# Prompt attention scores: the rotary query's high and low halves stacked on 128 partitions

## The chip, the cores and the metric

One core of a Trainium2 chip runs one inference step of one decoder layer as a single program. The metric is the device time of one execution, in microseconds (us); lower is better. The kernel before was timed in three runs, and one further execution was profiled.

## The reference

The layer has 512 prompt tokens and 8 sample sequences of 4 tokens each (544 columns in all). It runs a SwiGLU block, then two mixers side by side, a gated recurrence and a latent attention with 4 heads, then a second SwiGLU block. The change touches the prompt's scores of the latent attention alone. Its query has a part without position of 128 rows per head ("nope") and a rotary part of 64 rows per head; the rotary key of 64 rows is shared by all heads.

```python
qh = jnp.einsum('btc,chd->bthd', cq, w_q_up)
q_nope = qh[..., :QK_NOPE]                    # 128 per head
q_r = rope(qh[..., QK_NOPE:], pos)            # 64 per head
k_r = rope(kr[:, :, None, :], pos)[:, :, 0, :]  # 64, shared by the heads
...
s = (jnp.einsum('bqhr,bsr->bhqs', ql, c_kv) + jnp.einsum('bqhd,bsd->bhqs', qr, k_rope)) * scale
s = jnp.where(k_pos[None, None, None, :] <= qp[None, None, :, None], s, -jnp.inf)
p = jax.nn.softmax(s, axis=-1)
return jnp.einsum('bhqs,bsr->bqhr', p, c_kv)
```

For the prompt the kernel uses the expanded form: it computes keys and values of each head from the latent rows, so a score is nope query times nope key plus rotary query times rotary key.

## The kernel before

**Numbers in two halves.** A product of two float32 matrices is made of three products in a shorter float32 format (fp32r, shown as f32 by the profile). `split` makes a high half (a cast, on ACT, L168) and a low half (source minus high, on DVE, L169); for weights the same is done in L248 and L249. A product is then high·high + high·low + low·high; low·low is left out.

**The rotary query.** In the scope "at2" a loop over two head pairs g projects 128 rows (2 heads of 64), scales them into `qz` and calls `rope`. That copies four blocks of 32 rows into `rp_sw` with the halves swapped (ACT, L835), multiplies it (L836) and `qz` (L837) by the tables, and adds (L838, all DVE) into `qr`, 128 x 544. Then `split(qrh[:, g], qrl[:, g], qr)` gives the two halves, each with two heads on 64 partitions. Between these steps stand products for keys and values (accumulators `acc`, split by L168 and L169 into `uhb`/`ulb` and `Vh`/`Vl`).

**The rotary key.** The weight of the rotary key is loaded twice, so that `krT` holds the 64 rows on both halves of the partitions. Its halves are `Kh[:, 2]` and `Kl[:, 2]`.

**The scores.** `soft(hd, x)` makes the scores of head `hd` for half x of the prompt (256 queries): two groups, one for each tile of 128 queries. The group of query tile qt has N = 128·(qt+1) keys, so N is 128 and 256 for x = 0, and 384 and 512 for x = 1. With 4 heads there are 16 groups. A group is six products and one more: three of 128 rows (`qnh`, `qnh`, `qnl` against `Knh`, `Knl`, which lie in the buffers the profile calls `uhb` and `ulb`), three of 64 rows (`qrh`, `qrh`, `qrl` against `Kh`, `Kl`, called `ha` and `hb`), and a bf16 product with the identity (`idb`) that adds the causal mask `causb` (L1190). The first-named operand in a profile row s<-uhb,qnh is the one that streams; the query tile is the stationary weight. DVE then takes the maximum (L1195), ACT the exponential (L1199), PE transposes (`tp`, L1211), `split` makes `PTh`/`PTl`, and L1220 multiplies with the values into `o`.

**What sets the order.** A planner orders the instructions of each engine before the program is built; each engine then runs its list in order and waits on semaphores. Products of a later stage (projections, L257) are placed among the score groups. While heads of x = 0 end, `prep` weights (`w_q`, `wh`/`wl` of 128 x 768) are cast; while those of x = 1 run, output projections (`w_o`, 128 x 1024) and `decode_prep` (40 copies of `qsT`, half on ACT L1229, half on DVE L1231) run. After the last score group, gathers of cached pages start on POOL (L1354).

Of the kernel before, what the change touches and what calls it, by code (L numbers as in the profile page):

```python
# [9 lines left out]
F32R = mybir.dt.float32r  # L10
# [4 lines left out]
ALU = mybir.AluOpType  # L15
AX = mybir.AxisListType

P = 128
# [6 lines left out]
T = TP + TS  # L25
# [8 lines left out]
NH = 4  # L34
R = 256
RD = 64
# [72 lines left out]
def hybrid_step_kernel(  # L109
# [5 lines left out]
    nc = tc.nc  # L115
# [12 lines left out]
    def mk(shape, dt, tag, bufs=1, pool=None):  # L128
        return (pool or cur[-1]).tile(shape, dt, name=tag, tag=tag, bufs=bufs)

    @contextmanager
    def scope(name):
        with tc.tile_pool(name=name, bufs=1, reuse_waits="tile") as p_:
            cur.append(p_)
            yield p_
            cur.pop()
# [9 lines left out]
    def f32(ap):  # L146
        return ap.bitcast(F32)

    def actslot(name, x, dt=F32, shape=None, n=None):
        return mk(shape or [P, KD, n or HS[x]], dt, name + "ab"[x], pool=act)  # L150
# [13 lines left out]
    def gcol(j):  # L164
        return gv[:, j : j + 1]

    def split(hi, lo, src, eng=None):
        nc.scalar.copy(hi, src)  # L168
        (eng or nc.vector).tensor_tensor(lo, src, f32(hi), op=ALU.subtract)  # L169
# [603 lines left out]
    with scope("mix") as mx_:  # L773
# [39 lines left out]
        def more(n):  # L813
            for _ in some(n):
                pass
# [244 lines left out]
        with scope("at2"):  # L1060
            Vh = mk([P, 4, NH * P], F32R, "Vh")
            Vl = mk([P, 4, NH * P], F32R, "Vl")
            ukT = mk([P, NH, R], F32, "ukT")
            qrh = mk([P, 2, T], F32R, "qrh")
            qrl = mk([P, 2, T], F32R, "qrl")
            Q = [(qh[x], ql[x]) for x in BOTH]
            with scope("kv"):
                wkv = mk([P, 2, 1024], F32, "wkv")
                nc.sync.dma_start(wkv, w_kv.rearrange("(k p) f -> p k f", p=P))
                more(CQ[4])  # L1070
                s_kv = mk([P, T], F32, "s_kv")
                krT = mk([P, T], F32, "krT")
                for x, hs in enumerate(even):
                    nc.vector.tensor_tensor(krz[:, hs], krz[:, hs], U[x][2], op=ALU.mult)
                for x, hs in enumerate(even):
                    rstd(s_kv[:, hs], sumsq([zc[:, j, hs] for j in range(2)]), R, U[x][2])
                rope(krT, krz)
                ckT = mk([P, 2, T], F32, "ckT")
                for j in range(2):
                    nc.vector.scalar_tensor_tensor(ckT[:, j], zc[:, j], gcol(V_KVG + j), s_kv, op0=ALU.mult, op1=ALU.mult)  # L1080
                Kh = mk([P, 3, T], F32R, "ha", pool=act)
                Kl = mk([P, 3, T], F32R, "hb", pool=act)
                for j in range(3):
                    split(Kh[:, j], Kl[:, j], ckT[:, j] if j < 2 else krT)
                wk4 = wkv.rearrange("p k (h c) -> p k h c", h=NH)
                uk = mk([P, 2, 2, NH, P], F32R, "uk")
                for j in range(2):
                    split(uk[:, 0, j], uk[:, 1, j], wk4[:, j, :, :P])
                for g in range(2):
                    pu = ps("pu")  # L1090
                    for i in range(2):
                        for j in range(2):
                            nc.tensor.transpose(pu[:, (2 * i + j) * P : (2 * i + j + 1) * P], wk4[:, j, 2 * g + i, :P], ident)
                    nc.scalar.copy(ukT[:, 2 * g : 2 * g + 2], pu.rearrange("p (h r) -> p h r", h=2))
                more(9)
                uv = actslot("ul", 0, F32R, [P, 2, 2, NH * P])
                for j in range(2):
                    split(uv[:, 0, j].rearrange("p (h c) -> p h c", h=NH), uv[:, 1, j].rearrange("p (h c) -> p h c", h=NH), wk4[:, j, :, P:])
                Knh, Knl = (actslot(n, 1, F32R, [P, NH, TP]) for n in ("uh", "ul"))

                def keys(hd):
                    a = ps("acc", "acc")
                    mm3(a, [((uk[:, 0, j, hd], uk[:, 1, j, hd]), (Kh[:, j, :TP], Kl[:, j, :TP])) for j in range(2)])
                    split(Knh[:, hd], Knl[:, hd], a)

                def values(i):
                    a = ps("acc", "acc")
                    ts = slice(i * P, (i + 1) * P)
                    mm3(a, [((Kh[:, j, ts], Kl[:, j, ts]), (uv[:, 0, j], uv[:, 1, j])) for j in range(2)])
                    split(Vh[:, i], Vl[:, i], a)  # L1110

                for x in BOTH:
                    rstd(s_q[x], allsum(s_q[x]), QL, U[x][2])
                for g in range(2):
                    w = weight([w_qr[2 * g + i] for i in range(2)], KQ)
                    a = [gemm(w, Q[x]) for x in BOTH]
                    qz = mk([P, T], F32, "qz")
                    for x, hs in enumerate(even):
                        nc.vector.tensor_tensor(qz[:, hs], a[x], s_q[x], op=ALU.mult)
                    qr = mk([P, T], F32, "qr")  # L1120
                    rope(qr, qz)
                    split(qrh[:, g], qrl[:, g], qr)
                    for i in range(2):
                        nc.scalar.copy(qsT[0:RD, 2, :, :, 2 * g + i], qr[i * RD : (i + 1) * RD, TP:].rearrange("p (b t) -> p b t", b=NB))
                    keys(2 * g)
                    keys(2 * g + 1)
                for i in range(4):
                    values(i)
                po = ps("po")
                for j in range(2):  # L1130
                    nc.tensor.transpose(po[:TS, j * P : (j + 1) * P], ckT[:, j, TP:], ident)
                nc.vector.tensor_copy(cns, po[:TS, :R])
                nc.sync.dma_start(ckv_p, ckT[:, :, :TP])
                nc.sync.dma_start(kr_p, krT[0:RD, :TP])
                nc.sync.dma_start(ckv_s, cns)
                nc.sync.dma_start(kr_s, krT[0:RD, TP:])
                for j in range(2):
                    nc.vector.tensor_copy(kss[:, j], ckT[:, j, TP:])
                nc.vector.tensor_copy(kss[0:RD, 2], krT[0:RD, TP:])
# [26 lines left out]

            def soft(hd, x):
                qnh, qnl = qq[hd, x]
                r0 = (hd % 2) * RD
                q0 = 2 * x  # L1170
                ss = {}
                pe_t = mk([P, 896], F32, "pe", PEB)
                pes = {q0: pe_t[:, : (q0 + 1) * P], q0 + 1: pe_t[:, (q0 + 1) * P : (2 * q0 + 3) * P]}
                for qt in (q0, q0 + 1):
                    qs = slice(qt * P, (qt + 1) * P)
                    ls = slice((qt - q0) * P, (qt - q0 + 1) * P)
                    N = (qt + 1) * P
                    s = ss[qt] = ps("s")
                    n = 0
                    for j in range(2):  # L1180
                        if j == 0:
                            qa = (qnh[:, ls], qnl[:, ls])
                            ka = (Knh[:, hd, :N], Knl[:, hd, :N])
                        else:
                            qa = (qrh[r0 : r0 + RD, hd // 2, qs], qrl[r0 : r0 + RD, hd // 2, qs])
                            ka = (Kh[r0 : r0 + RD, 2, :N], Kl[r0 : r0 + RD, 2, :N])
                        for a_, b_ in ((0, 0), (0, 1), (1, 0)):
                            nc.tensor.matmul(s[:, :N], qa[a_], ka[b_], start=n == 0, stop=False, skip_group_check=True)  # L1188
                            n += 1
                    nc.tensor.matmul(s[:, qt * P : N], idb, causb, start=False, stop=True, skip_group_check=True)  # L1190
                for qt in (q0, q0 + 1):
                    N = (qt + 1) * P
                    s = ss[qt]
                    mx = mk([P, 1], F32, "mx", 2, pool=sb)
                    nc.vector.tensor_reduce(mx, s[:, :N], axis=AX.X, op=ALU.max)  # L1195
                    nc.vector.tensor_scalar_mul(mx, mx, -SCALE)
                    pe = pes[qt]
                    sm = mk([P, 1], F32, "sm", 2, pool=sb)
                    nc.scalar.activation(pe[:, :N], s[:, :N], AF.Exp, scale=SCALE, bias=mx, accum_out=sm)  # L1199
                    nc.vector.reciprocal(sm, sm)  # L1200
                    nc.vector.tensor_scalar_mul(pe[:, :N], pe[:, :N], sm)
                return pes
# [488 lines left out]
```

## Time and profile before

| what | value |
|---|---|
| median of three runs | 1271.8 us (1271.74 to 1272.26) |
| profiled execution | 1272.22 us, span 1270.4 us |
| mean granted TensorE clock | 0.994 |
| PE busy | 1250.7 us, 98% of the span, 12442 instructions |
| PE weight loads (PEld) | 1159.4 us, 91% |
| DVE / ACT / POOL busy | 982.6 / 741.2 / 75.9 us |
| score products of the prompt (L1188, L1190) | 112 products, between 629.2 and 701.2 us |

PE is the matrix engine, and PEld its weight loads, which overlap products; DVE, ACT, POOL and SP are the vector, scalar, general and DMA-issuing engines. A timeline row gives start and duration in us, engine, line, operation and out<-in; for PE then the tile, which is the part of the array that a product uses (rows*columns), and the shape of the streamed operand. "x2" joins neighbours of one kind, and brackets at the end give how long the engine stood idle before, and what it waited for. Ends of products are modelled and overlap the next start, so the cost of a product in a stream is read from start to start.

### The profile page before, as it was taken

How to read it: one execution, taken by the hardware profiler on the slowest of the kernel's cores; microseconds unless marked ns; L12 is line 12 of the kernel's file. 1: busy time of each engine (PE TensorE's matmuls, PEld its weight loads, DVE VectorE, ACT ScalarE, POOL GpSimd, SP SyncE). 2: the span in 40 equal slices, each digit the busy share in tenths (PEclk: the TensorE clock that was granted, in tenths of full speed). 3: DMA queues.
4: the chain of work that ended last, by engine and by line, in shares of the span. 5: the costliest groups of instructions: out<-in, count | busy, mean ns of one | idle time of the engine just before them, and what ended most of it. 6: DMA issues, size and time to landing. Idle time of an engine off the chain costs nothing.

```text
span 1270.4 us, 30188 instructions
## 1 busy us (share of the span) xinstructions
PE 1250.7 (98%) x12442; PEld 1159.4 (91%) x12442; DVE 982.6 (77%) x1972; ACT 741.2 (58%) x1560; POOL 75.9 (6%) x80
## 2 busy tenths in 40 slices
PE   8999999999999999999999999999999999999998
PEld 7999999999999988889888888788788999999996
DVE  7897778888678887767766898989987778566664
ACT  7665545454566644546557655664656776554454
POOL 0000000000000000000000422322300000000000
PEclk9999999999999999999999899999999999999998
DMA  6233323332254221223223978878676635545541
GB/s 233 84 117 100 100 84 100 101 100 92 54 218 157 78 90 59 80 78 127 80 85 102 345 254 298 286 263 316 240 267 209 193 113 178 189 133 187 157 144 49
DMA packets 73018, 195.08 MB, mean 154 GB/s; under 512 B 12368, under 2 KB 27760, under 8 KB 68144
## 3 DMA queue, kind: packets, MB, share of 16 engines
q1 hardware_dynamic: 64320, 149.88, 36.3%
q0 software_dynamic: 7168, 41.95, 9.0%
q8 instruction: 98, 1.61, 0.5%
q10 hardware_dynamic: 1392, 1.32, 0.4%
q14 instruction: 40, 0.33, 0.1%
HBM read 183.45 MB, written 9.67 MB: 152 GB/s over the span
## 4 chain that ended last, share of the span: by engine, by line
PE 88%; DVE 6%; ACT 5%; issue 1%; DMA 0%; SPq 0%; DVEq 0%; ACTq 0%
PE acc L257 29%; PE acc L275 18%; PE dn L257 8%; PE Y L559 6%; PE X L559 4%; PE Z L559 4%; PE s L1375 3%; PE acc L715 3%; PE o L1408 2%; DVE wl L249 1%; PE s L1188 1%; PE pa L931 1%; PE acc L286 1%; ACT wh L248 1%; DVE kh L1363 1%
## 5 line engine op out<-in xcount | busy, mean ns | idle before, releaser
L248 ACT CAST wh<-wraw 128x1024 fp32r<-128x1024 f32 (+2 forms) x194 | 185.1, 957 | 185.5 <-PE acc L257 117.9
L249 DVE TENSOR_TENSOR wl<-wraw,wh 128x1024 fp32r<-128x1024 f32 (+2 forms) x194 | 214.5, 1107 | 82.6 <-ACT wh L248 82.2
L275 PE MATMUL acc<-uha,wh 128*128 128x256 f32 (+1 forms) x528 | 159.3, 302 | 0.9 <-ACT uha L205 0.9
L275 PE MATMUL acc<-ula,wh 128*128 128x256 f32 (+1 forms) x528 | 151.5, 287 | 0.0
L275 PE MATMUL acc<-uha,wl 128*128 128x256 f32 (+1 forms) x528 | 150.3, 285 | 0.8 <-DVE wl L249 0.7
L257 PE MATMUL acc<-uhb,wh 128*128 128x288 f32 (+1 forms) x432 | 128.2, 297 | 0.0
L257 PE MATMUL acc<-ulb,wh 128*128 128x288 f32 (+1 forms) x432 | 127.5, 295 | 0.0
L257 PE MATMUL acc<-uhb,wl 128*128 128x288 f32 (+1 forms) x432 | 126.8, 295 | 0.6 <-DVE wl L249 0.3
L275 PEld LDWEIGHTS acc<-uha,wh 128*128 128x128 f32 x528 | 100.1, 190 | 15.2 <-issue 13.2
L275 PEld LDWEIGHTS acc<-uha,wl 128*128 128x128 f32 x528 | 100.1, 190 | 1.6 <-DVE wl L249 1.3
L275 PEld LDWEIGHTS acc<-ula,wh 128*128 128x128 f32 x528 | 100.5, 190 | 1.0 <-issue 1.0
L257 PEld LDWEIGHTS acc<-uhb,wl 128*128 128x128 f32 x432 | 81.2, 188 | 1.3 <-DVE wl L249 1.3
L257 PEld LDWEIGHTS acc<-uhb,wh 128*128 128x128 f32 x432 | 81.0, 187 | 0.7 <-ACT wh L248 0.3
L257 PEld LDWEIGHTS acc<-ulb,wh 128*128 128x128 f32 x432 | 81.1, 188 | 0.1
L257 PE MATMUL dn<-hh,dh 128*128 128x272 f32 x256 | 74.3, 290 | 0.0
L257 PE MATMUL dn<-hh,dl 128*128 128x272 f32 x256 | 73.7, 288 | 0.0
L257 PE MATMUL dn<-hl,dh 128*128 128x272 f32 x256 | 73.6, 288 | 0.0
L1399 ACT COPY pbuf<-pt 32x64 f32<-32x64 f32 x192 | 46.5, 242 | 13.3 <-DVE pt L1395 10.6
L1375 PE MATMUL s<-kh,q 64*32 64x128 f32 x2560 | 54.0, 275 | 0.0
L275 PE MATMUL acc<-uhb,wh 128*128 128x272 f32 x176 | 53.3, 303 | 0.0
L257 PE MATMUL acc<-hlb,wh 128*128 128x288 f32 x176 | 52.1, 297 | 0.0
L257 PE MATMUL acc<-hhb,wh 128*128 128x288 f32 x176 | 51.8, 298 | 0.0
(642 smaller groups left out, 3904.7 us busy)
## 6 DMA issues: line engine op xcount, KB each, us to landing
wraw<-w_u SPq DMA_DIRECT2D x66, 512.0 KB, 3.5
wraw<-w_g SPq DMA_DIRECT2D x65, 512.0 KB, 4.0
wraw<-w_d SPq DMA_DIRECT2D x40, 384.0 KB, 3.3
wraw<-w_in SPq DMA_DIRECT2D x24, 512.0 KB, 3.6
wraw<-w_d SPq DMA_DIRECT2D x32, 320.0 KB, 2.9
wraw<-w_d SPq DMA_DIRECT2D x16, 512.0 KB, 4.0
wraw<-w_o SPq DMA_DIRECT2D x16, 512.0 KB, 4.0
g_S<-state SPq DMA_DIRECT2D x4, 512.0 KB, 4.0
```

Of the source, the lines that this page charges most:

```text
L248: nc.scalar.copy(wh[:, :kt], w[:, :kt])
L249: nc.vector.tensor_tensor(wl[:, :kt], w[:, :kt], f32(wh[:, :kt]), op=ALU.subtract)
L257: nc.tensor.matmul(out, a, b, start=n == 0, stop=n == last)
L275: nc.tensor.matmul(acc[:, :n], a[:, k], b[:, k], start=k + i == 0, stop=k == kt - 1 and i == 2)
L286: nc.tensor.matmul(acc, a[:, k], b[:, k], start=k + i == 0, stop=k == kt - 1 and i == 2)
L559: nc.tensor.matmul(bank, a[p][:, k], b[q][:, k], start=first and k + n == 0, stop=k == 3 and n == 2, skip_group_check=True)
L715: nc.tensor.matmul(accs[x, d], wts[d][p][:, k], hs[k // 2][q][:, k % 2, x], start=k + n == 0, stop=k == nf - 1 and n == 2)
L931: nc.tensor.matmul(pa[es, c * 32 : (c + 1) * 32].rearrange("p (n m) -> p n m", m=m), kx[:, cs], up(qx[:, cs]), start=True, stop=True, skip ...
L1188: nc.tensor.matmul(s[:, :N], qa[a_], ka[b_], start=n == 0, stop=False, skip_group_check=True)
L1375: nc.tensor.matmul(self.s[r][c * 32 : c * 32 + 32, :P], q[rs, j], kh, start=st + jj == 0, stop=st == len(JS) - 1 and jj == 1, skip_group_c ...
L1399: (nc.scalar.copy if g else nc.vector.tensor_copy)(self.p[g * 32 : g * 32 + 32, c // 2, c % 2 * 4 : c % 2 * 4 + 4, self.i * 16 : self.i * ...
L1408: nc.tensor.matmul(o[g : g + 32, :R], self.p[:, c, a], self.craw[c][:, a], start=i + c == 0 and a < 4, stop=i + c == 2 and a >= 4, skip_gr ...
```

## The change

The tile pair `qrh`, `qrl` (each 128 x 2 x 544) is replaced by one tile `qr2` (128 x 4 x 544, the same size). For each head the cast writes the high half on the 64 partitions where its rows lie, and the subtract writes the low half on the other 64. As the key lies on both halves of the partitions, one product of 128 rows with `Kh` gives high·high + low·high, and one with `Kl` gives high·low + low·low. A group has two rotary products of 128 rows instead of three of 64, and a low·low term more.

```diff
-            qrh = mk([P, 2, T], F32R, "qrh")
-            qrl = mk([P, 2, T], F32R, "qrl")
+            qr2 = mk([P, NH, T], F32R, "qr2")
...
                     rope(qr, qz)
-                    split(qrh[:, g], qrl[:, g], qr)
+                    for i in range(2):
+                        a_, b_ = slice(i * RD, (i + 1) * RD), slice((1 - i) * RD, (2 - i) * RD)
+                        nc.scalar.copy(qr2[a_, 2 * g + i], qr[a_])
+                        nc.vector.tensor_tensor(qr2[b_, 2 * g + i], qr[a_], f32(qr2[a_, 2 * g + i]), op=ALU.subtract)
...
-                    for j in range(2):
-                        if j == 0:
-                            qa = (qnh[:, ls], qnl[:, ls])
-                            ka = (Knh[:, hd, :N], Knl[:, hd, :N])
-                        else:
-                            qa = (qrh[r0 : r0 + RD, hd // 2, qs], qrl[r0 : r0 + RD, hd // 2, qs])
-                            ka = (Kh[r0 : r0 + RD, 2, :N], Kl[r0 : r0 + RD, 2, :N])
-                        for a_, b_ in ((0, 0), (0, 1), (1, 0)):
-                            nc.tensor.matmul(s[:, :N], qa[a_], ka[b_], start=n == 0, stop=False, skip_group_check=True)
-                            n += 1
+                    kn, kr = ([t[:, j, :N] for t in ts] for ts, j in (((Knh, Knl), hd), ((Kh, Kl), 2)))
+                    qr = qr2[:, hd, qs]
+                    for a_, b_ in ((qnh[:, ls], kn[0]), (qnh[:, ls], kn[1]), (qnl[:, ls], kn[0]), (qr, kr[0]), (qr, kr[1])):
+                        nc.tensor.matmul(s[:, :N], a_, b_, start=n == 0, stop=False, skip_group_check=True)
+                        n += 1
```

The lines behind it move up, by four in `soft` and below (L1188 becomes L1184, L1190 becomes L1186, L1229 becomes L1225). On PE 16 products fall away. A group of N = 384 on PE, before:

```order
L1188 MATMUL s<-uhb,qnh 128x384
L1188 MATMUL s<-ulb,qnh 128x384
L1188 MATMUL s<-uhb,qnl 128x384
L1188 MATMUL s<-ha,qrh 128x384
L1188 MATMUL s<-hb,qrh 128x384
L1188 MATMUL s<-ha,qrl 128x384
L1190 LDWEIGHTS idb
L1190 MATMUL s<-causb,idb 128x128
```

The same group after (`qr_7262` is the tile `qr2`; the sizes here are those of the output):

```order
L1184 MATMUL s<-uhb,qnh 128x384
L1184 MATMUL s<-ulb,qnh 128x384
L1184 MATMUL s<-uhb,qnl 128x384
L1184 MATMUL s<-ha,qr_7262 128x384
L1184 MATMUL s<-hb,qr_7262 128x384
L1186 LDWEIGHTS idb
L1186 MATMUL s<-causb,idb 128x128
```

One rotary product is gone, and the causal product follows a product of 128 rows. The order of the other engines changes between some 615 and 705 us of the old trace. On DVE, around the first head pair's split, before:

```order
L838 TENSOR_TENSOR qr<-qr,rp_sw 128x544
L1119 TENSOR_TENSOR qz<-acc,s_q_4793 128x272
L1119 TENSOR_TENSOR qz<-acc,s_q_4794 128x272
L169 TENSOR_TENSOR qrl<-qr,qrh 128x544
L249 TENSOR_TENSOR wl<-wraw,wh 128x768
L837 TENSOR_TENSOR qr<-qz,trig 128x544
L836 TENSOR_TENSOR rp_sw<-rp_sw,trig 128x544
L169 TENSOR_TENSOR ulb<-acc,uhb 128x512
```

And after, the same place and the end of the stage:

```order
L838 TENSOR_TENSOR qr<-qr,rp_sw 128x544
L1118 TENSOR_TENSOR qz<-acc,s_q_4793 128x272
L1118 TENSOR_TENSOR qz<-acc,s_q_4794 128x272
L1124 TENSOR_TENSOR qr_7262<-qr,qr_7262 64x544 x2
L837 TENSOR_TENSOR qr<-qz,trig 128x544
L836 TENSOR_TENSOR rp_sw<-rp_sw,trig 128x544
L169 TENSOR_TENSOR ulb<-acc,uhb 128x512
L838 TENSOR_TENSOR qr<-qr,rp_sw 128x544
L169 TENSOR_TENSOR ulb<-acc,uhb 128x512
L169 TENSOR_TENSOR Vl<-acc,Vh 128x512
L1124 TENSOR_TENSOR qr_7262<-qr,qr_7262 64x544 x2
L169 TENSOR_TENSOR Vl<-acc,Vh 128x512 x3
```

Two subtracts of 64 rows stand for each one of 128, and the weight's `wl` has gone from here; it now stands behind the last `Vl` and the copy to `cns`, directly ahead of the first head's query. ACT's cast `wh` of the same weight moves with it. After that `wl` DVE now has two `ula` splits (128 x 256), the query half `qnl`, and two more `ula`; before, four `ula` came ahead of `qnl`.

On ACT, while the last groups of x = 1 are prepared (`qsT` copies are those of `decode_prep`, `wh` 128x1024 an output-projection weight), before:

```order
L1229 COPY q_8225<-qsT 32x128
L1199 ACTIVATE pe,sm<-s,mx 128x512
L1229 COPY q_8225<-qsT 32x128 x3
L248 CAST wh<-wraw 128x1024
L1229 COPY q_8225<-qsT 32x128 x3
L1222 COPY mb<-o 128x256
L768 COPY ma<-acc 128x256
L1238 COPY q_8225<-q_8225 32x10x16
L296 ACTIVATE ssp<-ma 128x256
L1238 COPY q_8225<-q_8225 32x10x16
L299 ACTIVATE ma<-ma,gv 128x256
L1238 COPY q_8225<-q_8225 32x10x16 x2
```

And after:

```order
L1225 COPY q_8218<-qsT 32x128
L1195 ACTIVATE pe,sm<-s,mx 128x512
L248 CAST wh<-wraw 128x1024
L768 COPY ma<-acc 128x256
L1225 COPY q_8218<-qsT 32x128
L296 ACTIVATE ssp<-ma 128x256
L1225 COPY q_8218<-qsT 32x128
L299 ACTIVATE ma<-ma,gv 128x256
L1218 COPY mb<-o 128x256
L1225 COPY q_8218<-qsT 32x128 x5
L1234 COPY q_8218<-q_8218 32x10x16 x4
L248 CAST wh<-wraw 128x1024
```

The weight cast comes ahead of three of the copies, and the copies go behind it; the set of instructions up to the next weight cast is the same. On PE the products that use these results move by a few places. POOL's order is the same, and on SP one store and one weight load change places.

More of the change, by code (lines that the diff above doesn't have):

```diff
@@ L1168, in soft @@
                 qnh, qnl = qq[hd, x]
-                r0 = (hd % 2) * RD
                 q0 = 2 * x
```

## The prediction

> **What bounds the kernel now.** I read the page first, its share of busy time and its chain, then the product timeline around the score groups, then the busy time of short stretches, and last PE's waits. From the page:
>
> ```profile
> PE 1250.7 (98%) x12442; PEld 1159.4 (91%) x12442; DVE 982.6 (77%) x1972; ACT 741.2 (58%) x1560; POOL 75.9 (6%) x80
> PE 88%; DVE 6%; ACT 5%; issue 1%; DMA 0%; SPq 0%; DVEq 0%; ACTq 0%
> ```
>
> PE is busy for 98% of the span and has 88% of the chain, so a microsecond that PE no longer needs is worth a microsecond, except in places where another engine ends last. The change touches PE from 629 to 701 us only. So I looked at that part in stretches (columns: length, then busy us and instructions of PE, weight loads, DVE, ACT and POOL, then the granted clock, DMA share and GB/s):
>
> ```profile
> 629.20:652.42 23.22, 23.22 (x181) 21.64 (x179) 14.49 (x46) 10.07 (x30) 0.00 (x0) 1.00 0.24 75
> 652.42:656.40 3.98, 3.86 (x30) 3.14 (x28) 3.90 (x13) 3.42 (x11) 0.63 (x1) 1.00 0.86 254
> 661.42:675.79 14.37, 13.32 (x93) 11.12 (x92) 11.81 (x40) 13.71 (x39) 0.00 (x0) 1.00 0.04 4
> 701.99:705.41 3.42, 2.38 (x16) 2.12 (x17) 2.39 (x8) 2.23 (x7) 2.81 (x4) 1.00 0.73 256
> 705.41:708.82 3.41, 1.94 (x15) 1.52 (x13) 2.54 (x5) 1.77 (x5) 2.94 (x3) 1.00 0.99 380
> 708.82:715.65 6.83, 6.41 (x29) 6.25 (x30) 6.69 (x15) 5.59 (x14) 2.02 (x3) 0.50 0.99 397
> ```
>
> From 629 to 652 PE has no idle time. In the next row DVE is full (3.90 of 3.98), and from 661.4 to 675.8 ACT is (13.71 of 14.37). There a shorter PE wins little. The last row matters for a rival: the clock is halved for 6.83 us.
>
> **What a score group costs now.** The product timeline of the two groups of the last head, N = 384 and 512 keys (start, modelled duration, tile, rows x columns):
>
> ```profile
> 698.20 0.34 PE L1188 MATMUL s<-uhb,qnl 128*128 128x384 f32 x1
> 698.47 0.44 PE L1188 MATMUL s<-ha,qrh 64*128 64x384 f32 x1
> 698.74 0.33 PE L1188 MATMUL s<-hb,qrh 64*128 64x384 f32 x1
> 698.92 0.34 PE L1188 MATMUL s<-ha,qrl 64*128 64x384 f32 x1
> 699.18 0.23 PE L1190 MATMUL s<-causb,idb 128*128 128x128 bf16 x1
> 699.22 0.48 PE L1188 MATMUL s<-uhb,qnh 128*128 128x512 f32 x1
> 699.54 0.39 PE L1188 MATMUL s<-ulb,qnh 128*128 128x512 f32 x1
> 699.77 0.39 PE L1188 MATMUL s<-uhb,qnl 128*128 128x512 f32 x1
> ...
> 701.05 0.39 PE L1211 MATMUL tp<-ident,pe 128*128 128x128 f32 x2
> ```
>
> The distance from one start to the next is what counts, since products overlap. Inside a run of equal tiles it is .18 at N = 384 (698.74 to 698.92) and .23 at 512 (699.54 to 699.77). Where the tile goes from 128*128 to 64*128 it is .27 (698.20 to 698.47), and again .27 behind the first 64-row product; where it goes back it is .26 (698.92 to 699.18). So each entry costs .09 + .09, and each exit .08 to .09. Rows do not shorten a product: 64 rows and 128 rows stream at the same distance. The small groups, N = 128 and 256:
>
> ```profile
> 629.37 0.28 PE L1188 MATMUL s<-uhb,qnl 128*128 128x128 f32 x1
> 629.57 0.32 PE L1188 MATMUL s<-ha,qrh 64*128 64x128 f32 x1
> 629.74 0.27 PE L1188 MATMUL s<-hb,qrh 64*128 64x128 f32 x1
> 629.85 0.27 PE L1188 MATMUL s<-ha,qrl 64*128 64x128 f32 x1
> 630.05 0.23 PE L1190 MATMUL s<-causb,idb 128*128 128x128 bf16 x1
> 630.09 0.36 PE L1188 MATMUL s<-uhb,qnh 128*128 128x256 f32 x1
> 630.29 0.28 PE L1188 MATMUL s<-ulb,qnh 128*128 128x256 f32 x1
> 630.41 0.29 PE L1188 MATMUL s<-uhb,qnl 128*128 128x256 f32 x1
> ...
> 631.22 0.50 PE L257 MATMUL acc<-q,wh 128*128 128x272 f32 x2
> ```
>
> Distances in stream: .11 at 128 (629.74 to 629.85), .12 at 256 (630.29 to 630.41).
>
> **Term 1, the groups.** After the change the three products qnl, stacked·ha, stacked·hb have one tile, and the causal product has it too. From the start of qnl to the start of what follows the causal product takes three stream distances and .04 (699.18 to 699.22):
> - N = 128: .72 (629.37 to 630.09) becomes .11×3 + .04 = .37, gain .35
> - N = 256: .81 (630.41 to 631.22) becomes .12×3 + .04 = .40, gain .41
> - N = 384: 1.02 becomes .18×3 + .04 = .58 (.56 unrounded), gain .45
> - N = 512: 1.28 becomes .23×3 + .04 = .73, with .03 for the wider step to the transposes .76, gain .52
>
> A head gains .76 in its first half (queries 0 to 255) and .97 in its second; four heads would be 6.9 us. One piece of this has no row: an f32 product of 128 rows followed by the bf16 causal product. The trace has only 64-row products ahead of it. Bounds: nothing extra (the step back from bf16 to f32 in one tile, .04), or all that the exit takes now, .09 ahead and up to .1 for uncovered weights. I take nothing, because its tile is 128*128 like its neighbours', and keep .2 for a rival. [...]
>
> **Term 2, the front.** The rotary queries are split twice, and the split now issues twice as many instructions:
>
> ```profile
> L168 ACT CAST qrh<-qr x2: 648/649/650, 615.7 to 622.3; 128x544 fp32r<-128x544 f32 x2
> L169 DVE TENSOR_TENSOR qrl<-qr,qrh x2: 714/720/726, 616.4 to 623.4; 128x544 fp32r<-128x544 f32 x2
> ```
>
> ```profile
> 611.11 2.61 ACT L835 COPY rp_sw<-qz 32x544 f32<-32x544 f32 x4
> 617.68 0.96 DVE L249 TENSOR_TENSOR wl<-wraw,wh 128x768 fp32r<-128x768 f32 x1 [0.54 <-ACT wh L248]
> 621.70 0.73 PE L257 MATMUL acc<-ula,ha 128*128 128x512 f32 x2 [0.39 <-DVE ulb L169]
> 626.16 1.07 DVE L169 TENSOR_TENSOR ula<-ma,uha 128x256 fp32r<-128x256 f32 x3
> 628.06 0.43 DVE L169 TENSOR_TENSOR qnl<-qn,qnh 128x256 fp32r<-128x256 f32 x1
> ```
>
> Four copies of 32 rows with 544 columns take 2.61, .65 each, as much as one of 128 rows. So a 64-row cast costs .65 and a 64-row subtract .72, and the change adds 2×.65 = 1.3 us on ACT and 2×.72 = 1.4 us on DVE between 615 and 624. A bound below would be half price, nothing added; above, I see no row dearer than these. The order moves a 768-wide weight's cast and subtract behind this place. On ACT that lets the second head pair's swap copies start some .2 to .3 earlier (a cast of .8 less, one of .65 and a start more), and on DVE the first pair's added .72 lies where .96 of the moved subtract and its wait of .54 were. So the wait of .39 at 621.70 shrinks by about .28 (ends 0 and .39). DVE then runs without a gap up to the first group's query half qnl, which ends at 628.49. Ahead of it come .72 (the second pair's added subtract) and the moved .96, behind it go two of the four output splits of .33 each: 628.49 + .72 + .96 − .66 − .28 = 629.23. PE first uses qnl at 629.37, with the .28 at 629.09: a wait of .14. I book the front at −.28 + .14 = −.14, with ends −.39 and +.4 (the .28 not won, and qnl that much later). The moved weight is needed at 631.6 and ready some 4 us before: 0, and the same 4 us are the cover. SP and POOL issue nothing more, and no DMA is added; SP's one swap, a store of the sample rows and a weight load far ahead of its use, I book at 0.
>
> **Term 3, what of term 1 arrives.** Heads 0 to 2, first halves, lie in the stretch without idle time: −3×.76 = −2.28. Head 3's first half lies beside the DVE-full stretch (652.4 to 656.4): its .76 is absorbed, PE would only wait longer for DVE. Then:
>
> ```profile
> 657.79 0.32 PE o L1220
> 658.11 0.54 PE s L1188 x2
> ```
>
> ```profile
> 661.42 0.27 ACT L1165 COPY qsT<-qa 128x64 f32<-128x64 f32 x1 [0.42 <-PE qa L1164]
> ```
>
> ```profile
> 666.67 0.66 PE L1211 MATMUL tp<-ident,pe 128*128 128x128 f32 x4 [0.36 <-ACT ma L1222]
> 668.74 0.39 PE L1220 MATMUL o<-PTh,Vh 128*128 128x256 f32 x1 [0.57 <-ACT PTh L168]
> 678.15 0.38 PE L257 MATMUL acc<-uha,wl 128*128 128x256 f32 x1 [0.35 <-DVE wl L249]
> ```
>
> The first two rows are of the chain, then ACT's timeline and PE's. Head 0's second half runs there, with an output product inside the 64-row run, which pays the switch twice more (.32 instead of .12 for it, .27 instead of .18 behind it: .3). So the 384 group gives .45 + .3 = −.75. From 661.42 ACT ends last: it waited .42 there, and then its work runs through (13.71 of 14.37, the rest being gaps of .03 between instructions). The .52 of the 512 group lets ACT start earlier by at most that wait: −.42. Head 1's second half (661.7 to 665.8) then only lengthens PE's waits at 666.67 and 668.74; its .97 is absorbed. The order shifts some of ACT's copies behind a weight cast, but the set up to the next cast (675.8) is the same, so that cast ends no later; DVE's half follows at 678.15 and PE goes on from there. Heads 2 and 3, second halves, lie in PE's stream (680 to 684, 697.9 to 701.1): −2×.97 = −1.94.
>
> Behind 701 PE waits for exp, its transpose and its split, a chain of fixed length that starts with the last group, and the gather on POOL starts with the last score product too:
>
> ```profile
> POOL ulb L1354 <- PE s L1188: 47.1, 1, 47.1
> ```
>
> So the tail moves as a whole, and from 709 to the end PE is the bound. The sum: −.14 −2.28 −.75 −.42 −1.94 = −5.53. The profiled execution took 1272.22; that gives 1266.7, and against the median of the runs (1271.8, .4 less) 1266.3.
>
> **Rivals.**
> (a) *The causal product still drains.* For: no row shows that pair. Against: it has the same tile. Of the 16 groups 11 count above (three first halves with two each, one, two second halves with two each), at .09 to .2: 1.0 to 2.2 us back, 1267.3 to 1268.5.
> (b) *The halved clock goes.* The clock fell at 708.82 behind two stretches of 3.4 us in which PE was busy 2.38 and 1.94, and came back after 6.83. Granted clock seems to follow how busy PE was in stretches of 3.4 us; if these waits, moved by 5.5 us, spread over three of them, each is busier, and up to half of 6.83 comes back: 3.4. Against: DMA is at .99 of its share there, so the weights behind would end last, and I expect 0 to 2 of it: 1264.3 to 1266, at best 1262.9. [...]
> (c) *The change doesn't do what it says*: the .27 steps belong to the query buffer, not to the tile, and only the 16 products go. Against: the step back to bf16 shows it too. Then 3×(.11+.12) + .18 + 2×(.18+.23) = 1.7 arrives, with the front and ACT's wait 2.3: 1269.5 to 1270.1, no change that one can tell.
> (d) *Slower: the clock is halved in the ACT-full stretch.* Heads 0 and 1 leave about 1.1 us more idle time on PE between 661 and 676 (.97 and .1), on top of 1.05 (14.37 less 13.32 busy). Busy falls from .93 to .85; the halving at 708 followed .70 and .57. Halved work of PE costs half its length, so it decides from 11 us on (2×5.5): the 6.83 seen, three times over, from 657 to 677, would cost 10.2 and give 1276.5. Far from the rows, a small chance.
>
> **How the numbers follow.** My forecast, .53: 1266.3, its own range 1265 to 1267.2. (a) .17, (b) .18, (c) .09, (d) .03. About .2%, 2.5 us, is what a measurement of this kernel can tell from no change, so the line lies at 1269.3. (a), (b) and the forecast are faster (.88); (c) is the same (.09); (d) slower (.03). The range leaves out (c), (d) and the best end of (b): 1263.0 to 1269.0.
>
> **What the profile of after should show.** No 64*128 tile in the score rows; five products a group; steps of .18 throughout at N = 384, and .58 or less from qnl to the product behind the causal one. The step ahead of the causal product decides (a). The wait of PE at 621.70 falls to about .1, with about as much at the first group. PE's waits at 666 and 668 grow to about 2 us together, and the start of the wait-free stream behind 678 comes 3.6 us earlier, the last score product 5.5 us earlier. The clock rows from 700 to 716 decide (b), those from 661 to 678 (d). I would be wrong by most if the DVE-full stretch moved on with PE, or ACT's copies, now behind the cast, made PE wait longer than the absorbed gains.

## Result: faster by 0.2%, 3.2 us instead of 5.5

The changed kernel takes 1268.51 us (median of 14 runs, 1266.72 to 1270.88), the kernel before 1271.67 (14 runs): ratio 0.9978, 95% interval 0.9971 to 0.9985 (the quotient of the two medians, 0.9975, lies inside). The profiled execution of the change took 1267.03 us, 1.5 less than the median; that of before was 0.6 above its median. So the two traces differ by 5.2 us and the medians by 3.2, and the difference between these two numbers is the subject of what follows. From the page of after:

```profile
PE 1243.1 (98%) x12426; PEld 1155.6 (91%) x12426; DVE 982.9 (78%) x1974; ACT 742.1 (59%) x1562; POOL 79.0 (6%) x80
PE 86%; DVE 6%; ACT 5%; issue 1%; DMA 1%; SPq 0%; DVEq 0%; ACTq 0%
```

PE has 16 products fewer and is 7.6 us less busy; the span is 5.1 us shorter, and the rest became waits. The product timeline of the last two groups in after:

```profile
694.16 0.33 PE L1184 MATMUL s<-uhb,qnl 128*128 128x384 f32 x1
694.33 0.33 PE L1184 MATMUL s<-ha,qr 128*128 128x384 f32 x1
694.50 0.34 PE L1184 MATMUL s<-hb,qr 128*128 128x384 f32 x1
694.68 0.23 PE L1186 MATMUL s<-causb,idb 128*128 128x128 bf16 x1
694.72 0.48 PE L1184 MATMUL s<-uhb,qnh 128*128 128x512 f32 x1
...
695.27 0.40 PE L1184 MATMUL s<-uhb,qnl 128*128 128x512 f32 x1
...
695.96 0.23 PE L1186 MATMUL s<-causb,idb 128*128 128x128 bf16 x1
696.03 0.94 PE L1207 MATMUL tp<-ident,pe 128*128 128x128 f32 x7
```

From qnl to what follows the causal product it is .56 at N = 384 and .76 at 512, as worked out. The step from the 128-row f32 product to the bf16 causal product is .18 (694.50 to 694.68), a stream step, where before took .26 behind a 64-row product (698.92 to 699.18): rival (a), .09 to .2 more there, is refuted. The first group and PE's waits up to 676 us:

```profile
621.99 0.73 PE L257 MATMUL acc<-ula,ha 128*128 128x512 f32 x2 [0.33 <-DVE ulb L169]
629.55 0.27 PE L1184 MATMUL s<-ulb,qnh 128*128 128x128 f32 x1
629.84 0.33 PE L1184 MATMUL s<-uhb,qnl 128*128 128x128 f32 x1
...
661.71 0.38 PE L1216 MATMUL o<-PTh,Vh 128*128 128x256 f32 x1 [0.26 <-ACT pe L1195]
664.05 0.65 PE L1207 MATMUL tp<-ident,pe 128*128 128x128 f32 x4 [0.74 <-ACT ma L1218]
673.83 0.38 PE L257 MATMUL acc<-uha,wh 128*128 128x256 f32 x1 [0.35 <-ACT wh L248]
675.10 0.39 PE L257 MATMUL acc<-uha,wl 128*128 128x256 f32 x1 [0.76 <-DVE wl L249]
```

The wait at 622 hardly shrank (.33 after .39), and the first qnl comes .18 late (.29 behind the product ahead of it, instead of .11). From 661 to 676 PE waits 2.1 us in four places; before it was 1.3 in three, up to 678 (.36, .57 and .35, shown in the prediction). Most of the gain of head 1 went there.

The causal products mark the stages. The first one starts at 630.05 before and 630.23 after, the last at 700.98 and 695.96: the stage is 70.93 and 65.73 us long, 5.20 less. Both starts of the program differ by .34 (an early product, 605.12 and 605.46), so up to the last score product the change wins 5.36. The forecast had 5.53.

### The profile page after: what moved, and what is told of

The parts are those of the page before. It is cut to its first block, busy times and chain, and to the rows that moved or that the text cites. A ratio compares the mean times of both kernels' runs of the same rounds, so it can differ in the third digit from the quotient of the medians.

```text
span 1265.3 us, 30161 instructions
## 1 busy us (share of the span) xinstructions
PE 1243.1 (98%) x12426; PEld 1155.6 (91%) x12426; DVE 982.9 (78%) x1974; ACT 742.1 (59%) x1562; POOL 79.0 (6%) x80
## 4 chain that ended last, share of the span: by engine, by line
PE 86%; DVE 6%; ACT 5%; issue 1%; DMA 1%; SPq 0%; DVEq 0%; ACTq 0%
PE acc L257 30%; PE acc L275 17%; PE dn L257 8%; PE Y L559 6%; PE X L559 4%; PE Z L559 4%; PE acc L715 3%; PE s L1371 3%; PE o L1404 2%; DVE wl L249 1%; ACT wh L248 1%; PE pa L931 1%; DMA wraw<-w_g 1%; PE acc L286 1%; DVE kh L1359 1%
```

## Experiments

The kernels ran on three chips: on one (the chip of the parts and of the copies on POOL; the first result took the same time) the kernel before takes 1271.6, on the two others 1283.4 and 1282.6 (there the decode stage takes 250 to 252 us instead of 239 to 240). Ratios are always to runs of the kernel before on the same chip.

**How the two kernels spread.** No edit.

> The kernel before, unchanged, to see how its own runs spread. Theory 1 (the halved clock behind the last score group is the cause of the spread): its runs fall into groups by granted clock, 0 to 3 stretches of 3.4 us halved, each worth about 1.7 us, and most of them have the two stretches of the profile (clock 0.994): spread about 1270 to 1273, ratio 1.000. Theory 2 (the spread is the start and the DMA, not the clock): span and granted clock are not related.

> The changed kernel, unchanged. Theory 1: ratio 0.997 to 0.998 again, spans of 1264.7 at clock 0.997 up to 1268 at 0.993, so the spread of 4 us goes with the clock, and the profile shows a number of halved stretches between 697 and 715 us that fits its own span. Theory 2: spans of one clock differ as much as spans of different clocks.

Measured: 1.0001 (0.9992 to 1.0010) and 0.9976 (0.9966 to 0.9986). The stage from the first to the last causal product was 70.89 and 65.73 us. Time goes with clock, though not in steps as neat as theory 1 had it: in 35 runs of before on the chip where it takes 1271.6 the correlation of span and granted clock is -0.81 (spans 1267.8 to 1270.3 at 0.997 to 0.999, 1270.3 to 1273.1 at 0.993 and 0.994); on the chip of these two runs it is only -0.48.

**Unused products in PE's waits.** In `value`, ahead of the output products:

```diff
                 o = ps("o")
+                with tc.issue_after(last_tp.ins) if x and hd > 1 else nullcontext():
+                    for _ in range((0, 0, 5, 4)[hd] * x):
+                        nc.tensor.matmul(o, Vh[:, 0, hs], Knh[:, hd], start=True, stop=True, skip_group_check=True)
```

> The changed kernel with nine products of 512 columns whose result is not used, five between the last-but-one head's transposes and its first output product, four at the same place of the last head, where PE waits 1.25 and 0.96 us in the profile. Theory 1: the two 3.4 us stretches there are busy enough, the halved clock goes in most runs, the median falls by 1 to 2 us to about 1266.7, and the spread to about 1 us. Theory 2: the products lie in waits, so the median stays at 1268.5 with the same spread; if they are in the way, up to 0.5 us slower.

> The kernel before with the same nine unused products. Theory 1: its two halved stretches go too, 1271.7 falls to between 1268.5 and 1270, and the distance to the changed kernel with the same products is what the score groups alone are worth, 5 to 5.7 us if the halved clock is gone from both, or about 3.2 us if it costs both the same. Theory 2: stays at 1271.7.

Measured: 0.9967 (0.9955 to 0.9979) with the change, 1.0002 (0.9993 to 1.0011) without it. Theory 1 fails in its times: without the change nothing was won, though no run of 11 had a clock below 0.9955, and with the change the median is only 0.4 us under the change's own on that chip (1.0 when it was repeated on the third), which the intervals do not tell from nothing. One reason stands in the trace: the five products did not fill the first wait. The timeline of a later run of the same kernel:

```profile
698.26 1.42 PE L1215 MATMUL o<-uhb,Vh 128*128 128x512 f32 x5 [1.25 <-ACT pe L1195]
```

They need no probabilities and yet waited 1.25 us for ACT's exponential, which reads a score tile. The author took it that they wait for the buffer of `o`, which a score tile held until then; no run shows which buffer it is. The products behind them lie on the path. In the kernel before the same five products waited .72 us, for DVE's maximum (L1196) and not for ACT; the maximum reads a score tile too.

**The change in parts.** Three edits: the stacked product by the low key issued twice (to the change); the third rotary product left out (to before); each split in two pieces of 64 rows (to before).

```diff
-...(qr, kr[0]), (qr, kr[1])):
+...(qr, kr[0]), (qr, kr[1]), (qr, kr[1])):
```

```diff
-                        for a_, b_ in ((0, 0), (0, 1), (1, 0)):
+                        for a_, b_ in ((0, 0), (0, 1), (1, 0))[: 3 - j]:
```

```diff
-                    split(qrh[:, g], qrl[:, g], qr)
+                    for i in range(2):
+                        a_ = slice(i * RD, (i + 1) * RD)
+                        split(qrh[a_, g], qrl[a_, g], qr[a_])
```

> The changed kernel with the stacked product by the low key issued twice, so three rotary products of 128 rows (the low key counts twice in the scores). The number of products is that of before, the tile switch is gone. Theory A (what is won at the last score product arrives whole at the end): the last causal product starts 3.5 to 3.7 us earlier than before (5.36 of the change less 1.7 for the products) and the time falls by as much. Theory B (some 1.5 to 2 us of any gain are given back behind the last score product, since work there does not start earlier with it): 3.6 us earlier at the last score product, about 2 us at the end. Rival C (the buffer, not the tile, made the .27 steps): no gain at all.

> The kernel before without the third rotary product, low query by high key (that term is left out): two rotary products of 64 rows in a group, the tile switch stays, and so does the old split. Theory A: 1.7 us earlier at the last score product and 1.7 us at the end. Theory B: 1.7 at the last score product, 0 to 1 at the end. Rival C: 5 us, as in the change.

> The kernel before with each rotary split made in two pieces of 64 rows, written to the old tiles, three products of 64 rows as before: the change's cost on ACT and DVE alone, with its moved weight cast. By the prediction 0 to 0.4 us slower at the first score group (-0.14 was booked with a wait of 0.14 at the first group); theory A: the same at the end, so a ratio of 1.0000 to 1.0003; theory B: no difference at the end.

Measured, stage from the first to the last causal product and ratio:

| kernel | stage, us | won | ratio |
|---|---|---|---|
| no tile switch, same count | 68.38 | 2.55 | 0.9981 (0.9973 to 0.9990), median -2.2 us |
| two products, switch stays | 68.86 | 2.07 | 1.0003 (0.9994 to 1.0012), median +0.2 us |
| split in pieces | 70.86 | .07 | 0.9999 (0.9990 to 1.0008), median +0.1 us |

Rival C is out: without the tile switch, and with as many products as before, the last score product comes 2.55 us earlier. The expectation of 3.6 there was too high; the two parts add up to 4.62, .58 less than the change, and where that is lost was not traced. Neither theory holds for both: by the medians the first kernel keeps what it won, the second loses it all. So the loss is not the same for every gain ahead of the tail; the kernels differ in something. PE's first two waits behind the last group, in the kernel without the switch and in that with two products:

```profile
701.28 0.36 PE L1216 MATMUL o<-PTh,Vh 128*128 128x256 f32 x1 [0.90 <-DVE mx L1192]
701.84 0.39 PE L1216 MATMUL o<-PTl,Vh 128*128 128x256 f32 x1 [0.21 <-DVE PTl L169]
```

```profile
701.70 0.38 PE L1220 MATMUL o<-PTh,Vh 128*128 128x256 f32 x1 [1.25 <-ACT pe L1199]
702.54 0.39 PE L1220 MATMUL o<-PTl,Vh 128*128 128x256 f32 x1 [0.46 <-DVE PTl L169]
```

And the same in before, and then in after with the two waits that follow:

```profile
702.80 0.36 PE L1220 MATMUL o<-PTh,Vh 128*128 128x256 f32 x1 [0.81 <-DVE mx L1196]
703.38 0.39 PE L1220 MATMUL o<-PTl,Vh 128*128 128x256 f32 x1 [0.23 <-DVE PTl L169]
```

```profile
698.21 0.38 PE L1216 MATMUL o<-PTh,Vh 128*128 128x256 f32 x1 [1.25 <-ACT pe L1195]
699.06 0.39 PE L1216 MATMUL o<-PTl,Vh 128*128 128x256 f32 x1 [0.46 <-DVE PTl L169]
702.77 0.39 PE L1216 MATMUL o<-PTh,Vh 128*128 128x256 f32 x1 [0.96 <-ACT PTh L168]
704.91 0.79 PE L275 MATMUL acc<-uha,wh 128*128 128x256 f32 x2 [0.93 <-ACT uha L205]
```

The change and the two-product kernel wait 1.71 us in the first two; before waits .81 + .23 = 1.04, the kernel without the switch 1.11. DVE's timeline shows why. Before:

```profile
699.01 1.22 DVE L249 TENSOR_TENSOR wl<-wraw,wh 128x1024 fp32r<-128x1024 f32 x1 [1.29 <-ACT wh L248]
700.15 0.42 DVE L298 TENSOR_TENSOR ssp<-ssp,sq 128x256 f32<-128x256 f32 x1
700.49 0.55 DVE L1195 TENSOR_REDUCE mx<-s 128x1 f32<-128x384 f32 x1
701.25 0.69 DVE L1195 TENSOR_REDUCE mx<-s 128x1 f32<-128x512 f32 x1 [0.21 <-PE s L1190]
...
702.09 0.56 DVE L169 TENSOR_TENSOR PTl<-tp,PTh 128x384 fp32r<-128x384 f32 x1
...
702.64 0.69 DVE L169 TENSOR_TENSOR PTl<-tp,PTh 128x512 fp32r<-128x512 f32 x1
```

After:

```profile
694.95 0.56 DVE L1191 TENSOR_REDUCE mx<-s 128x1 f32<-128x384 f32 x1 [1.27 <-PE s L1186]
695.42 1.21 DVE L249 TENSOR_TENSOR wl<-wraw,wh 128x1024 fp32r<-128x1024 f32 x1
696.56 0.42 DVE L298 TENSOR_TENSOR ssp<-ssp,sq 128x256 f32<-128x256 f32 x1
...
696.96 0.68 DVE L1191 TENSOR_REDUCE mx<-s 128x1 f32<-128x512 f32 x1
697.55 0.54 DVE L169 TENSOR_TENSOR PTl<-tp,PTh 128x384 fp32r<-128x384 f32 x1
...
698.32 0.68 DVE L169 TENSOR_TENSOR PTl<-tp,PTh 128x512 fp32r<-128x512 f32 x1
```

With shorter groups the planner put the first maximum ahead of a weight's low half (`wl`, `ssp`), 1.5 us of work that DVE ended .5 us before the last causal product, and ends .9 us behind it now. DVE first waited 1.27 us for PE; then the maximum of the last group starts 1.00 us behind its causal product (.27 before), and the previous head's two splits into PTl end 3.04 behind it (2.35 before). The kernel with two products has the same order; its maximum starts .71 behind the causal product (699.45), and its splits too end 3.04 behind it:

```profile
698.15 0.56 DVE L1195 TENSOR_REDUCE mx<-s 128x1 f32<-128x384 f32 x1 [1.56 <-PE s L1190]
698.62 1.21 DVE L249 TENSOR_TENSOR wl<-wraw,wh 128x1024 fp32r<-128x1024 f32 x1
...
700.16 0.68 DVE L1195 TENSOR_REDUCE mx<-s 128x1 f32<-128x512 f32 x1
```

In the change the order is only a part of it, though. `wl` needs ACT's `wh`. Where DVE waited for that, `wl` started 1.08 us behind the start of `wh`, and in after `wh` started at 693.88:

```profile
697.93 1.05 ACT L248 CAST wh<-wraw 128x1024 fp32r<-128x1024 f32 x1 [0.54 <-PE acc L257]
```

```profile
693.88 1.05 ACT L248 CAST wh<-wraw 128x1024 fp32r<-128x1024 f32 x1 [0.54 <-PE acc L257]
```

So `wl` could not have started before 694.96, where the first maximum starts now. From the start of `wh` to the last causal product it is 2.08 us now (3.05 before), since the two groups are .97 shorter, and DVE has the same work to do behind `wh`. In the kernel without the switch, which has the old order, it takes 3.81 us from the start of `wl` to the end of the splits (697.98 to 701.79). By that, as an estimate, the old order would have ended them at 698.77 in the change and not at 699.00: some .2 of the .69 us belong to the order and the rest to the shorter groups. In the kernel with two products `wl` could have started at 697.87, and by the same estimate the order makes up all of the .69.

The longer waits cost .5 directly, as the next numbers show. Then the clock. From the last causal product to the first decode product the traces take the following times (us), by how long the clock was halved there:

| DVE order | 3.4 us halved | 6.8 us | 10.2 us |
|---|---|---|---|
| old | 24.4 (split in pieces, no switch) | 25.5 (before) | 27.0 (before run again, twice) |
| new | 24.9 (after, the change run again, copies on POOL) | 26.4 (the change on the third chip) | 26.3 (two products) |

A further 3.4 us at half clock cost .7 to 1.5 us. These ten traces do not show more halved time with the new order than with the old one; for that the mean clock over all runs is needed, below.

```profile
698.13:701.55 3.42, 2.88 (x21) 2.58 (x21) 1.71 (x6) 1.64 (x6) 2.81 (x4) 1.00 1.00 381
701.55:704.96 3.41, 1.51 (x12) 1.10 (x10) 3.00 (x6) 1.78 (x6) 2.94 (x3) 1.00 0.98 387
704.96:708.37 3.41, 3.41 (x15) 3.19 (x16) 3.41 (x9) 2.12 (x7) 2.80 (x3) 0.50 1.00 420
```

These are stretches of after (columns as in the prediction): the halved one follows one in which PE was busy 1.51 of 3.41. The two-product kernel had three halved stretches in a row:

```profile
704.07:714.31 10.24, 9.56 (x40) 8.44 (x40) 8.14 (x16) 6.81 (x16) 5.37 (x6) 0.50 1.00 416
```

**Copies off ACT.** The one edit that tests the place where head 1's gain is absorbed:

```diff
-                            nc.scalar.copy(qrep[g * 32 : g * 32 + 32, j], src)
+                            (nc.gpsimd.tensor_copy if j < 6 else nc.scalar.copy)(qrep[g * 32 : g * 32 + 32, j], src)
```

> The changed kernel with 12 of the 20 ACT copies of the decode query (L1225) put on POOL. If ACT is what absorbs head 1's gain between 661 and 676 us, PE's waits there (0.26, 0.74, 0.35 and 0.76 in the profile of the change) shrink and the last score product comes 1 to 2 us earlier than in the change; theory A then gives 1 to 2 us at the end, theory B 0 to 1. If POOL's copies are slow (over 1 us each), they hold up the tail instead and it is up to 3 us slower.

Measured: 0.9977 (0.9965 to 0.9990), the stage 65.83 us: nothing won. PE's waits there became one:

```profile
665.31 0.66 PE L1207 MATMUL tp<-ident,pe 128*128 128x128 f32 x4 [2.08 <-ACT ma L1218]
```

2.08 + .27 at 661.5 is 2.35, more than the 2.1 of the change. But this does not clear ACT, since ACT now waited for the copies ahead of the same head's exponential:

```profile
659.00 4.46 POOL L1225 COPY q<-qsT 32x128 f32<-32x128 f32 x12 [7.33 <-ACT PTh L168]
663.15 0.67 ACT L1234 COPY q<-q 32x160 f32<-32x160 f32 x2 [1.40 <-POOL q L1225]
```

By the profile POOL took .37 us for each of the 12 copies (ACT .30); ACT's copies from their results (L1234) had to wait for the last, and the exponential of 384 columns behind them started at 663.84 (662.61 in the change). So the edit put POOL in the place of ACT's copies, and whether ACT alone binds this stretch stays open.

**Once more, on the third chip.**

> The changed kernel once more, for its stages and its spread. From the traces so far: first causal to last causal product 65.7 us (70.9 before), last causal product to first decode product 24.9 where 3.4 us there are halved, and 1 us more for each further 3.4. Theory D (the 5.4 us arrive at the last score product in every run, and about 2 are lost behind it, where PE now waits .67 us longer and the clock is halved for longer): stages as said, and runs below clock 0.996 are 1.5 to 3 us longer than the others. Theory E (the gain itself varies from run to run): the first stage differs from 65.7 by a microsecond or more.

> The kernel before once more. Theory D: first to last causal product 70.9, from there to the first decode product 24.4 with 3.4 us halved, 25.5 with 6.8, 26.3 to 27 with 10.2. Theory E: the first stage differs from 70.9 by a microsecond or more.

> The changed kernel with the nine unused products in its two waits, again. Theory D: mean granted clock higher than that of the changed kernel in the same call (0.997 against 0.995), ratio .0005 to .0015 lower, few runs more than 2 us above its fastest. Otherwise the same ratio as the changed kernel.

> The changed kernel with 16 unused products of 32 columns in the first of the two waits, some 0.4 us of PE time, so that PE has as many products as before. Theory D: too little work for the clock, so clock and time as the changed kernel. Theory F (with 16 products fewer, the time around the span, 1.8 us in nearly all runs of before, is 2 to 3 us in some runs of the change and of the two-product kernel: it goes with the number of PE instructions): that time is 1.8 in all runs here, and the median 0.3 us lower than the changed kernel's.

Measured: the change 0.9972 (0.9961 to 0.9984), before 1.0004, fill 0.9965 (0.9951 to 0.9978), 16 small products 0.9983 (0.9973 to 0.9993). The stage is 65.78 and 70.90: theory E is out, the gain at the last score product is the same in every trace (seven with the change 65.72 to 65.83, five with before's products 70.86 to 70.96, with the old split or the new). The small products are in the way, like the five above (their group starts at 698.17 behind the same 1.25 us and takes 1.96, not the .4 that was expected). The time around the span was 1.8 us in all of these runs with the change, so theory F finds nothing to explain here: it had been 2.0 to 3.0 in 9 of 14 runs of the change at first, and in 3 of 9 later, and 2.0 to 3.3 in 6 of 11 runs of the two-product kernel and in 5 of 12 with the copies on POOL. In all runs of before it is under 1.92. What that is stays open; it makes up .3 us of the mean of the first result. Theory D had runs of the change below clock 0.996 as 1.5 to 3 us longer than the others; here they are .5 longer (spans).

Mean granted clock over all runs, and runs below 0.9955:

| DVE order at the last group | kernels | mean clock | below 0.9955 |
|---|---|---|---|
| old | before (106 runs), no switch, split in pieces | 0.9959 to 0.9971 | 32 of 128 |
| new | the change (30 runs), copies on POOL, two products, 16 small products | 0.9948 to 0.9954 | 37 of 64 |
| with nine unused products | before and change | 0.9968 to 0.9972 | 0 of 22 |

Where before takes 1271.6 the change has 0.9952 and before 0.9962, on the two other chips 0.9954 and 0.9949 against 0.9966 and 0.9967. A mean of .0010 to .0018 less is 1.3 to 2.3 us of full clock over 1270 us, if all the halved time were PE's to lose. Within the kernels the runs show less: a clock lower by .001 goes with .58 us more span where before takes 1271.6, and with .38 on the two other chips. So an estimate of the clock's share is .5 to 2.3. With the .5 of the longer wait the balance is -5.4 + .5 + .5 to 2.3 = -4.4 to -2.6 for the change (medians -3.2, -3.5 and -3.2), and for two products, with .0014 less, -2.1 + .5 + .8 to 1.8 = -.8 to +.2 (median +.2); for no switch, with the clock of before, -2.5 (median -2.2). The balance can close, but its bounds are wide. The lower mean clock of the kernels with the new order is measured. That the order of DVE, or the longer waits, causes it is argued: no run has an edit of that order alone.

## Why the prediction was right, and where it was not

- **Term 1 (groups)** held to .02: .56 and .76 for N = 384 and 512, and the step ahead of the causal product is .18, with nothing added. Rival (a) is refuted. What it calls a drain shows in before as a step of .26 instead of .18; what PE does in that time no run shows.
- **Term 2 (front)** was booked at -.14 and is +.13: the wait at 622 fell by .06 instead of .28, and the first qnl came .18 late (booked .14). The 64-row instructions cost what the 128-row ones do (.72 us for a subtract of either size, .64 and .65 for a cast).
- **Term 3** was right in its sum (5.36 of 5.53 at the last score product) and, as far as the runs show, in its reason: head 1's gain was absorbed about where it was said (waits of 1.3 became 2.1, though half of them lie at 673.8 and 675.1 and not at 666 and 668), beside an ACT that was busy for 14.07 of 14.58 us from 661.42 to 676.00. That ACT is the limit there no run has tested, since with the copies on POOL it waited for POOL.
- **The step that failed** is "Behind 701 PE waits for exp, its transpose and its split, a chain of fixed length that starts with the last group ... So the tail moves as a whole". The chain doesn't start with the last group alone: it runs through DVE's queue, where `wl` hangs on an earlier cast of ACT and didn't move up with the groups, and where the change had put `wl` and `ssp` between the two maxima. The splits into PTl end 3.04 us behind the last causal product instead of 2.35. That was to be read from the order of before and after, with the 1.2 us of `wl` and the 1.29 us that DVE waited ahead of it.
- **Rival (b)** had the clock as a possible gain of up to 3.4 us. It went the other way: over all runs a low clock is more frequent with the new order (37 of 64 runs against 32 of 128), and by the balance above (.5 to 2.3 us) it may be the larger part of the loss. That the waits, .67 us longer, are the reason is argued, not shown, and that the granted clock follows how busy PE was in stretches of 3.4 us was the author's estimate: halved stretches came behind 1.51 to 2.38 us busy, but other stretches with 2.16 to 2.88 were followed by a clock of 1.00.
- **Rival (c)** is refuted by the kernel without the switch (2.55 us for the switch alone). **Rival (d)** did not happen: the clock is 1.00 in every step of 3.41 us between 657 and 677 us in the traces of before and after.
- The time lies inside the range (1263.0 to 1269.0), .5 under its end, but 2.2 us above the forecast of 1266.3 and outside the forecast's own range (1265 to 1267.2). It is at the end of rival (a)'s range (1268.5), whose mechanism is refuted, so the number alone would have pointed at the wrong cause. That the profiled execution (1267.03) came nearer to the forecast is partly luck: 3.4 us were halved behind its last score product, and 6.8 in the profile of before.

## What to carry to other kernels

A product of 64 rows streamed no faster here than one of 128 rows (.18 us at 384 columns), and going to its tile and back cost some .26 us a group; stacking two halves on 128 partitions removes both the switch and a product. A gain on the bounding engine should be followed past the last instruction that becomes shorter. Work of another engine that hangs on an earlier event does not move up with it, and a planner that sees shorter work may put a long, unurgent instruction between two short ones on which the path waits; both are read from the queue of the engine that ends the next wait, here DVE. Before an engine is cleared by moving its work elsewhere, see whether it now waits for the new place. Where the granted clock differs from run to run, compare medians of many runs with the trace: the one profiled execution lay 1.5 us off.

## What the runs showed of the hardware

- In after a 128-row f32 product followed by a bf16 product of the same tile keeps the stream step (.18 at 384 columns); the change of tile in the trace of before costs .09 on the step to 64 rows, .09 on the step behind it, and .08 to .09 on the way back.
- In the nine traces that were followed in steps of 3.41 us between 692 and 718 us, a stretch of half clock lasted one, two or three such steps (3.41, 6.83 and 10.24 us). The step ahead of a halved stretch had PE busy for 1.51 to 2.38 us; other steps with 2.16 to 2.88 were not followed by half clock. The busy time by the profile alone does not separate the two.
- The chips differ by 0.9% on the same kernel (medians of before 1271.6 against 1283.4 and 1282.6 us), nearly all of it in the decode stage (239 to 240 against 250 to 252 us).
